# Weight-stationary jobs of a two-layer hybrid decoder: three products of 256 columns per k tile in one PSUM bank, in place of 512 and 256 columns in two

## The chip, the cores and the metric

The kernel runs on one core of a Trainium2 chip, in one launch. The metric is the device time of one execution in microseconds (us). The kernel before takes 1260.89 us (median of 3 runs, 1260.34 to 1261.17). Matrix products run on TensorE (PE in the profile; its weight loads are PEld), elementwise work on VectorE (DVE), ScalarE (ACT) and GpSimd (POOL). SyncE (SP) issues most loads. PSUM is the memory that TensorE writes to, in banks of 128 x 512 float32.

## The reference

Two layers over 256 tokens of width 1024. Each layer has a mixer and a SwiGLU network, both on RMS-normed input, both added to the running h:

```
def hybrid_mixer(h, w_in, ...):
    u = h @ w_in
    q, k, v, g_ret, z, xbc, dt, gate_ret, gate_ssd = split(u)
    qf, kf = rotary(q), rotary(k) * DK ** -0.5
    yr = silu(g_ret) * norm(retention(qf, kf, v))
    o_ret = yr @ ret_out
    xbc = silu(causal_dwconv(xbc, conv_w, conv_b))
    xs, bm, cm = split(xbc)
    ys = ssd_scan(xs * dtp, dtp * a, bm, cm) + d_skip * xs
    o_ssd = (groupnorm(ys * silu(z)) * ssd_norm_w) @ ssd_out
    return (sigmoid(gate_ret) * o_ret + sigmoid(gate_ssd) * o_ssd) @ w_o

def swiglu(h, w_gate_up, w_down):
    gate, up = split(h @ w_gate_up)
    return (silu(gate) * up) @ w_down
```

A last RMSNorm follows. All is float32. There are 4 retention heads (256 wide q and k, 512 wide v), 32 SSD heads in 4 groups, and the SwiGLU width is 2816.

## The kernel before

**Products in three parts.** A float32 operand is split into a high part, rounded to float32r, and the low rest, and a product is the sum of three: high by high, high by low, low by high (`mm3`, L538). Activations are split once. Weights are split after they land, 128 x 1024 elements at a time, in `split_piece` (L490): ScalarE rounds `wh` (L502), VectorE takes `wl = raw - wh` (L523). A pair wh, wl occupies one of `HB` = 6 split slots (semaphore `hlS`, L258) from the rounding until its last product. Raw tiles (`RB` = 4) are loaded by SP in a fixed order (`feeder`, L474). In some jobs a sum of two weight tiles is made by a GpSimd DMA that adds in place (L412).

**Two kinds of job on TensorE.** In a tm job (`tm_jobs`, L801) tokens are stationary: the 128 x 128 weights of the array come from the transposed activations, and 512 columns of wh or wl stream past, with the lines L539, L540, L541 of `mm3`. The jobs `seven` (L840) do the same with seven products for eight (Strassen's scheme). In an fm job (`fm_job`, L944) the weight tile is stationary and the 256 tokens stream, so that the output stands channel by row: q and k (for the rotary turn), the convolution's channels (xs and bc), and three blocks of the SwiGLU. There are 30 fm jobs in a layer, 60 in all. Each makes 256 channels as two blocks (b) of 128, and each block runs over 8 k tiles. The activation tile holds high and low part side by side, `x = [xh | xl]`, so that one matmul of 512 columns does wh by both:

```
if k < 7:
    nc.tensor.matmul(a, lhsT=wh[..], rhs=x[..], ...)           # L962, 512 columns
nc.tensor.matmul(a[:, :SEQ], lhsT=wl[..], rhs=xh[..], ...)     # L963, 256 columns
if k == 7:
    nc.tensor.matmul(a, lhsT=wh[..], rhs=x[..], ...)           # L965, 512 columns
```

A block thus fills a whole bank: the left half has wh xh + wl xh, the right half wh xl. `gathered` (L980) adds the halves: ScalarE copies the right one out, VectorE adds the left one, and the bank is released. This is done for block 0 while block 1 runs. Then come the steps of the job's kind: `rotary` (L1357, VectorE), `conv` (L1456: one ScalarE step and three VectorE steps per block, then one Silu), or `gate` and `up` of `fm_pair` (L1830). A variant `fm_direct` (L920) with three products of 256 columns is in the code and is used by no job (`DIRECT = ()`, L1120).

**What sets the order.** All engines' queues are written out by a planner that runs when the kernel is built (`Flow`, L72). Every step is a stream that yields operations with an engine, a cost in ns and a priority (the smaller goes first); the planner simulates the engines with these costs and emits each operation when its engine would take it. So a cost or a delay in the planner changes only the order in which instructions stand in the queues. On the chip each engine takes its queue strictly in that order and waits where an operand isn't there. There are 6 banks for products (`accS`, L255), 2 for transposes (`trS`, L256) and 2 large scratch tiles (`ccS`, L259).

**Around the merge.** At the end of `ssd_out`, `ssd_post` (L1743) gates each 128 x 512 block of the sum on VectorE (`D<-acc,D`), adds the retention branch (`D<-D`), and `transposed` (L627) lets TensorE transpose it (L636) for the product with `w_o`, whose first products follow. `transposed` has an argument `slack`: a delay in the planner, after the transpose bank is taken, before TensorE is asked; some callers give `SLOW` = 1500 ns. In `z_job` (L1712) the sums for the seven products of `ssd_out` have the priority of the job plus `ZS_PR` = 1.0.

Of the kernel before, what the change touches and what calls it, by code (L numbers as in the profile page):

```python
# [11 lines left out]
AF = mybir.ActivationFunctionType  # L12
ALU = mybir.AluOpType
# [179 lines left out]
def trunk_kernel(  # L193
# [3 lines left out]
    ssd_out, w_o, norm_ffn_w, w_gate_up, w_gf, w_sw, w_dw, w_down, final_norm_w, consts, out,  # L197
):
    nc = tc.nc
    HB, RB, TAIL, WARM = 6, 4, 5, 2  # L200
    APART, LATE = (), 2500.0
    SLOW = 1500.0
    ZS_PR = 1.0
    PR0, SLACK = 1.6, 2500.0
    BESIDE = (8, 10, 12, 14, 11, 11, 9, 24, 44)
    APARTS, SUMS_PR = {}, 3.5
# [21 lines left out]
    def tt(n, pr, out, in0, in1, op):  # L228
        return dve(n, pr, lambda: nc.vector.tensor_tensor(out=out, in0=in0, in1=in1, op=op))  # L229
# [14 lines left out]
    def pe(cost, pr, fn):  # L244
        return Op("pe", cost, fn, pr)

    def mm_cost(n, fp32=False):
        return n * 4 / 2.4 + 4 if fp32 else max(n / 2.4 + 13.4, 110)
# [668 lines left out]
        for q in jobs[j]:  # L917
            yield from product(q)

    def fm_direct(xT, post):  # L920

        j, pe_pr = take()
        evs = jobs[j]
        box = []
        yield accS
        for b in range(2):
            fsl, to = slice(b * P, (b + 1) * P), slice(b * SEQ, (b + 1) * SEQ)
            for k in range(8):
                for t in range(NT):
                    yield xT.ready[k // 4][t]  # L930
                wh, wl = yield evs[k // 4]

                def emit():
                    if not box:
                        box.append(new_acc())
                    xh, xl = xT.at(k // 4)[:2]
                    mm3(box[0][:, to], wh[:, k % 4, fsl], wl[:, k % 4, fsl], xh[:, k % 4, :], xl[:, k % 4, :], k == 0, k == 7)

                yield pe(3 * mm_cost(256), pe_pr + 0.5, emit)
                if b == 1 and k % 4 == 3:  # L940
                    fl.release(hlS)
        fl.spawn(post(box[0], None, j))

    def fm_job(xT, post):  # L944

        j, pe_pr = take()
        evs = jobs[j]
        second = Event()
        for b in range(2):
            fsl = slice(b * P, (b + 1) * P)  # L950
            yield accS
            ps = None
            for k in range(8):
                for t in range(NT):
                    yield xT.ready[k // 4][t]
                wh, wl = yield evs[k // 4]

                def emit():
                    a = new_acc() if ps is None else ps
                    xh, _, x = xT.at(k // 4)  # L960
                    if k < 7:
                        nc.tensor.matmul(a, lhsT=wh[:, k % 4, fsl], rhs=x[:, k % 4, :, :], start=k == 0, stop=False)  # L962
                    nc.tensor.matmul(a[:, :SEQ], lhsT=wl[:, k % 4, fsl], rhs=xh[:, k % 4, :], start=False, stop=False)  # L963
                    if k == 7:
                        nc.tensor.matmul(a, lhsT=wh[:, k % 4, fsl], rhs=x[:, k % 4, :, :], start=False, stop=True)  # L965
                    return a

                ps = yield pe(mm_cost(512) + mm_cost(256) + 5, pe_pr + 0.5, emit)
                if b == 1 and k % 4 == 3:
                    fl.release(hlS)  # L970
            if b == 0:
                fl.spawn(post(ps, second, j))
            else:
                fl.set(second, ps)

    def halves(a):
        a = a.rearrange("p (i b t) -> p i b t", i=2, b=2)
        return a[:, 0, :, :], a[:, 1, :, :]

    def gathered(ps, u, pr):  # L980

        yield act(SEQ, pr, u, ps[:, SEQ:], AF.Copy, psum=True)
        yield tt(SEQ, pr, u, ps[:, :SEQ], u, ALU.add)
        fl.release(accS)

    def out_job(op, nk, post, head=0):

# [43 lines left out]
    def out_wino(op, nk, at, tag, order, post, add, ops):  # L1031
# [72 lines left out]
        for t in range(NT):  # L1104
# [12 lines left out]
           [("fm", 3)],  # L1117
           [("seven", (4,), ("t3", "t4"))],
           [("fm", NPAIR)]]
    DIRECT = ()  # L1120
    DOWN_APART = ()


# [75 lines left out]
    def layer(l, mix, nxt, opening=None):  # L1199
# [155 lines left out]
        ret_ev = [Event() for _ in range(RH)]  # L1355

        def rotary(dst, done):  # L1357
            def post(ps, second, j):
                d = yield dst
                yield ccS  # L1360
                tcx, tsx = halves(new_cc())
                yield from gathered(ps, tcx[:, 0, :], j)
                ps = yield second
                yield from gathered(ps, tcx[:, 1, :], j)
                yield tt(512, j, tsx, tcx, sin.unsqueeze(1).broadcast_to([P, 2, SEQ]), ALU.mult)
                yield tt(512, j, tcx, tcx, cos.unsqueeze(1).broadcast_to([P, 2, SEQ]), ALU.mult)
# [86 lines left out]
        run["q"], run["k"] = q_job, k_job  # L1453


        def conv(ps, second, blk, dst, pr):  # L1456
            cv, _ = yield par
            yield ccS
            u, cvt = halves(new_cc())

            def col(i, b):
                return cv[:, i, blk + b : blk + b + 1]

            for b in range(2):
                if b:
                    ps = yield second
                yield from gathered(ps, u[:, b, :], pr)
                yield act(SEQ, pr, cvt[:, b, :], u[:, b, :], AF.Identity, scale=col(3, b), bias=col(4, b))
                for i in range(1, 4):
                    yield stt(SEQ - i, pr, cvt[:, b, i:], u[:, b, : SEQ - i], col(3 - i, b), cvt[:, b, i:], ALU.mult, ALU.add)  # L1470
            yield act(512, pr, dst, cvt, AF.Silu)
            fl.release(ccS)

# [1 line left out]
        bc_ev = [[Event(), Event()] for _ in range(2)]  # L1475

        def bc_post(w, jj):
            def post(ps, second, j):
# [4 lines left out]
                yield from conv(ps, second, 16 + 4 * w + 2 * jj, d[:, 2 * jj : 2 * jj + 2, :], j)  # L1483
                fl.set(bc_ev[w][jj])
            return post

# [11 lines left out]
        cb_left = [SG]  # L1498

        def xs_post(g, jj):  # L1500
            def post(ps, second, j):
# [6 lines left out]
                yield from conv(ps, second, 4 * g + 2 * jj, sT, j)  # L1508
                yield trS
                yield SLOW  # L1510

# [231 lines left out]
        def ssd_post(t, n, ps, j):  # L1743
            nsl = slice(n * 512, (n + 1) * 512)
            yield sgs_ev[t][n]
            yield tt(512, j - 1, sgs[t][:, nsl], ps, sgs[t][:, nsl], ALU.mult)
            fl.release(accS)
            yield mr_ev[t][n]
            yield tt(512, j - 1, sgr[t][:, nsl], sgr[t][:, nsl], sgs[t][:, nsl], ALU.add)
            yield from transposed(sgr[t][:, nsl], 4, mT, n, t, j - 1)  # L1750
            if n == 1:
                fl.release(bigS["D"])
                fl.release(bigS["D"])
# [76 lines left out]
        def fm_pair(c):  # L1830
# [3 lines left out]
            for half in range(left[0]):  # L1834
                gated = Event()

                def summed(ps, second, u, j):
                    for b in range(2):
                        if b:
                            ps = yield second  # L1840
                        yield from gathered(ps, u[:, b * SEQ : (b + 1) * SEQ], j)

                def gate(ps, second, j, gated=gated):
                    yield silS
                    s = new_sil()
                    if second is None:
                        yield act(512, j, s, ps, AF.Silu, psum=True)
                        fl.release(accS)
                    else:
                        yield from summed(ps, second, s, j)  # L1850
                        yield act(512, j, s, s, AF.Silu)
                    fl.set(gated, s)

                def up(ps, second, j, gated=gated, half=half):
                    if second is None:
                        s = yield gated
                        yield tt(512, j, s, ps, s, ALU.mult)
                        fl.release(accS)
                    else:
                        yield sxS  # L1860
                        u = new_sx()
                        yield from summed(ps, second, u, j)
                        s = yield gated
                        yield tt(512, j, s, u, s, ALU.mult)
                        fl.release(sxS)
                    yield from gu.take(c)
                    dh, dl = (a[:, 2 * half : 2 * half + 2, :] for a in gu.at(c)[:2])
                    v = s.rearrange("p (b t) -> p b t", b=2)
# [5 lines left out]
                        for t in range(NT):  # L1874
                            fl.set(gu.ready[c][t])

                job = fm_direct if c in DIRECT else fm_job
                makers += [((lambda p=p, job=job: job(ffn.xT, p)), 1) for p in (gate, up)]
            return makers

        def pair(c):
# [211 lines left out]
```

## Time and profile before

| | before |
|---|---|
| median of 3 runs | 1260.89 us |
| profiled execution, its own time | 1260.23 us |
| its span, first to last instruction | 1258.2 us |
| VectorE busy | 1062.3 us, 84% |
| ScalarE busy | 851.0 us, 68% |
| granted TensorE clock, mean | 0.999 |

A matmul's record lasts longer than the array is taken by it, since matmuls overlap in the pipeline: records of 512 columns last 400 ns and start every 227 ns or so. How long TensorE is taken by a matmul is therefore read from the distance between starts (the pitch), and idle time of TensorE below some 0.17 us does not show in the busy sums. In the rows of the timeline the first two numbers are start and length in us; neighbours of the same kind are merged into one row with their count.

### The profile page before, as it was taken

Reading aid. Unit: us, or ns where it says so; the run is one execution under the profiler, and the core shown is the slowest. Engines: PE = TensorE matmul, PEld = TensorE weight load, DVE = VectorE, ACT = ScalarE, POOL = GpSimd, SP = SyncE. Lnnn points to the kernel's source line nnn. Section 1 sums busy time; section 2 is a strip of 40 time slices with the busy share of each in tenths; the row PEclk is TensorE's granted clock in tenths of the full one; section 3 lists DMA queues with packets and bytes.
Section 4 is the critical chain, followed back from the end, with each engine's and each line's share of the span. In section 5 each row is a group of like instructions: output and inputs, shape, how many; then the busy total and the mean of one; then the engine's idle time right before and its main releaser. Section 6 shows DMA issues by size and latency. Waiting matters only on the chain.

```text
span 1258.2 us, 17517 instructions
## 1 busy us (share of the span) xinstructions
PE 1247.1 (99%) x6306; PEld 1055.3 (84%) x6306; DVE 1062.3 (84%) x1452; ACT 851.0 (68%) x1271; POOL 64.4 (5%) x84
## 2 busy tenths in 40 slices
PE   9999999999999999999999999999999999999997
PEld 7889888888888788888888898888888887888886
DVE  6998978878589978999788888878875998888996
ACT  6876786987376566776586676967954664766754
POOL 0000000000012001011000000000000110010010
PEclk9999999999999999999999999999999999999999
DMA  8668555555475757886766485555555765678873
GB/s 292 222 176 292 178 175 160 175 189 196 154 281 148 230 177 225 296 225 207 229 210 226 123 266 166 172 192 167 187 199 170 242 189 201 206 226 254 271 202 113
DMA packets 73606, 258.13 MB, mean 205 GB/s; under 512 B 8464, under 2 KB 8720, under 8 KB 73520
## 3 DMA queue, kind: packets, MB, share of 16 engines
q1 hardware_dynamic: 66832, 233.32, 54.6%
q0 software_dynamic: 6400, 23.18, 9.8%
q8 instruction: 49, 0.80, 0.2%
q10 hardware_dynamic: 288, 0.52, 0.1%
q14 instruction: 37, 0.30, 0.1%
HBM read 255.88 MB, written 1.11 MB: 204 GB/s over the span
## 4 chain that ended last, share of the span: by engine, by line
PE 86%; DVE 8%; DMA 3%; issue 2%; ACT 1%; SPq 0%; POOL 0%; POOLq 0%; ACTq 0%; DVEq 0%
PE acc L540 17%; PE acc L539 17%; PE acc L541 17%; PE acc L962 16%; PE acc L963 9%; DVE wl L523 4%; PE tr L636 2%; PE acc L965 2%; PE yps L1623 2%; DVE raws L229 1%; DMA raws<-in_w_sw_dram 1%; DMA raw<-in_w_dw_dram 1%; DMA raw<-in_ssd_out_dram 1%; DVE D L229 1%; DVE plain L229 1%
## 5 line engine op out<-in xcount | busy, mean ns | idle before, releaser
L523 DVE TENSOR_TENSOR wl<-raw,wh 128x1024 fp32r<-128x1024 f32 (+2 forms) x392 | 464.5, 1194 | 76.1 <-ACT wh L502 73.7
L502 ACT ACTIVATE wh<-raw 128x1024 fp32r<-128x1024 f32 (+2 forms) x392 | 400.9, 1036 | 186.2 <-PE acc L541 87.3
L962 PE MATMUL acc<-xT,wh 128*128 128x512 f32 x840 | 304.1, 400 | 0.0
L963 PE MATMUL acc<-xT,wl 128*128 128x256 f32 x960 | 252.2, 281 | 0.0
L539 PE MATMUL acc<-wh,xT 128*128 128x512 f32 (+1 forms) x568 | 219.5, 386 | 0.0
L541 PE MATMUL acc<-wh,xT 128*128 128x512 f32 (+1 forms) x568 | 216.0, 380 | 0.0
L540 PE MATMUL acc<-wl,xT 128*128 128x512 f32 (+1 forms) x568 | 216.0, 380 | 0.0
L963 PEld LDWEIGHTS acc<-xT,wl 128*128 128x128 f32 x960 | 181.2, 189 | 10.1
L962 PEld LDWEIGHTS acc<-xT,wh 128*128 128x128 f32 x840 | 158.0, 188 | 32.3
L540 PEld LDWEIGHTS acc<-wl,xT 128*128 128x128 f32 x568 | 106.7, 188 | 20.1 <-issue 1.0
L539 PEld LDWEIGHTS acc<-wh,xT 128*128 128x128 f32 x568 | 106.7, 188 | 19.5 <-issue 1.2
L541 PEld LDWEIGHTS acc<-wh,xT 128*128 128x128 f32 x568 | 106.7, 188 | 19.5
L502 ACT ACTIVATE wh<-raws 128x1024 fp32r<-128x1024 f32 x80 | 84.1, 1057 | 45.1 <-DVE raws L229 23.6
L523 DVE TENSOR_TENSOR wl<-raws,wh 128x1024 fp32r<-128x1024 f32 x80 | 96.3, 1218 | 9.2 <-ACT wh L502 9.1
L539 PE MATMUL acc<-wh,A 128*128 128x512 f32 x224 | 89.0, 397 | 0.0
L541 PE MATMUL acc<-wh,A 128*128 128x512 f32 x224 | 87.3, 390 | 0.0
L540 PE MATMUL acc<-wl,A 128*128 128x512 f32 x224 | 87.2, 389 | 0.0
L232 DVE SCALAR_TENSOR_TENSOR cc<-cc,cv 128x255 f32<-128x255 f32 (+1 forms) x144 | 68.3, 477 | 11.5 <-ACT cc L222 10.4
L539 PE MATMUL acc<-wh,C 128*128 128x512 f32 (+1 forms) x184 | 72.2, 392 | 0.0
L540 PE MATMUL acc<-wl,C 128*128 128x512 f32 (+1 forms) x184 | 71.2, 387 | 0.5 <-DVE wl L523 0.3
L541 PE MATMUL acc<-wh,C 128*128 128x512 f32 (+1 forms) x184 | 70.7, 384 | 0.0
L541 PEld LDWEIGHTS acc<-wh,A 128*128 128x128 f32 x224 | 42.1, 188 | 9.0
(183 smaller groups left out, 1889.0 us busy)
## 6 DMA issues: line engine op xcount, KB each, us to landing
raw<-in_w_tm_dram SPq DMA_DIRECT2D x104, 512.0 KB, 4.2
raw<-in_w_fm_dram SPq DMA_DIRECT2D x80, 512.0 KB, 4.0
raw<-in_w_gf_dram SPq DMA_DIRECT2D x40, 512.0 KB, 4.7
raw<-in_ret_out_dram SPq DMA_DIRECT2D x32, 512.0 KB, 3.8
raw<-in_w_gate_up_dram SPq DMA_DIRECT2D x32, 512.0 KB, 6.0
raw<-in_w_down_dram SPq DMA_DIRECT2D x28, 512.0 KB, 4.4
raw<-in_w_gr_dram SPq DMA_DIRECT2D x24, 352.0 KB, 3.8
seg<-acs SPq DMA_DIRECT2D x16, 512.0 KB, 5.1
```

What stands on the lines that cost most here:

```text
L229: return dve(n, pr, lambda: nc.vector.tensor_tensor(out=out, in0=in0, in1=in1, op=op))
L232: return Op("dve", 1.04 * n + 130, lambda: nc.vector.scalar_tensor_tensor(out=out, in0=in0, scalar=scalar, in1=in1, op0=op0, op1=op1), pr)
L502: nc.scalar.activation(out=wh[:, :m], in_=raw[:, :m], func=AF.Copy)
L523: nc.vector.tensor_tensor(out=wl[:, :m], in0=raw[:, :m], in1=wh[:, :m].bitcast(F32), op=ALU.subtract)
L539: nc.tensor.matmul(ps, lhsT=lh, rhs=rh, start=first, stop=False, **kw)
L540: nc.tensor.matmul(ps, lhsT=lh, rhs=rl, start=False, stop=False, **kw)
L541: nc.tensor.matmul(ps, lhsT=ll, rhs=rh, start=False, stop=last, **kw)
L636: nc.tensor.transpose(out=ps[:, j * P : (j + 1) * P], in_=src[:, j * P : (j + 1) * P], identity=ident)
L962: nc.tensor.matmul(a, lhsT=wh[:, k % 4, fsl], rhs=x[:, k % 4, :, :], start=k == 0, stop=False)
L963: nc.tensor.matmul(a[:, :SEQ], lhsT=wl[:, k % 4, fsl], rhs=xh[:, k % 4, :], start=False, stop=False)
L965: nc.tensor.matmul(a, lhsT=wh[:, k % 4, fsl], rhs=x[:, k % 4, :, :], start=False, stop=True)
L1623: nc.tensor.matmul(ps[:, i * HD : (i + 1) * HD], lhsT=sg[:, i, :], rhs=xdt[:, i * HD : (i + 1) * HD], start=True, stop=True)
```

## The change

- `fm_job` and `gathered` go; `fm_direct` takes the name `fm_job` and does all 60 jobs. Each k tile is wh xh, wh xl, wl xh of 256 columns each, all into one half of one bank; block 1 uses the other half. The step that reads the result is spawned once, after both blocks. The planner's cost of a k tile is 3 * 117 = 351 ns (for the pair before: 352).
- The steps read the bank itself: `rotary` multiplies by sin and cos from PSUM, `conv` reads PSUM in its ScalarE step and its three VectorE steps per block, `gate` and `up` read PSUM. The bank is released after the last of these reads.
- `HB` goes from 6 to 7 split slots (8 KB more in each partition), and the scratch memory for the descriptors of GpSimd's DMAs is set to 8192 bytes (`dynamic_dma_scratch_size`).
- The transposes of the merged sum get `slack = MT_SLACK` = 800 ns.
- `ZS_PR` goes from 1.0 to 0.5.

```
-    HB, RB, TAIL, WARM = 6, 4, 5, 2
+    HB, RB, TAIL, WARM = 7, 4, 5, 2
-    SLOW = 1500.0
-    ZS_PR = 1.0
+    SLOW, MT_SLACK = 1500.0, 800.0
+    ZS_PR = 0.5
...
-    def fm_direct(xT, post):
+    def fm_job(xT, post):
         j, pe_pr = take()
         evs = jobs[j]
         box = []
         yield accS
         for b in range(2):
             fsl, to = slice(b * P, (b + 1) * P), slice(b * SEQ, (b + 1) * SEQ)
             for k in range(8):
...
                     xh, xl = xT.at(k // 4)[:2]
                     mm3(box[0][:, to], wh[:, k % 4, fsl], wl[:, k % 4, fsl], xh[:, k % 4, :], xl[:, k % 4, :], k == 0, k == 7)
-                yield pe(3 * mm_cost(256), pe_pr + 0.5, emit)
+                yield pe(3 * 117, pe_pr + 0.5, emit)
                 if b == 1 and k % 4 == 3:
                     fl.release(hlS)
-        fl.spawn(post(box[0], None, j))
+        fl.spawn(post(box[0], j))
...
-    def gathered(ps, u, pr):
-        yield act(SEQ, pr, u, ps[:, SEQ:], AF.Copy, psum=True)
-        yield tt(SEQ, pr, u, ps[:, :SEQ], u, ALU.add)
-        fl.release(accS)
...
         def rotary(dst, done):
-            def post(ps, second, j):
+            def post(ps, j):
                 d = yield dst
                 yield ccS
                 tcx, tsx = halves(new_cc())
-                yield from gathered(ps, tcx[:, 0, :], j)
-                ps = yield second
-                yield from gathered(ps, tcx[:, 1, :], j)
-                yield tt(512, j, tsx, tcx, sin.unsqueeze(1).broadcast_to([P, 2, SEQ]), ALU.mult)
-                yield tt(512, j, tcx, tcx, cos.unsqueeze(1).broadcast_to([P, 2, SEQ]), ALU.mult)
+                x = ps.rearrange("p (b t) -> p b t", b=2)
+                yield tt(512, j, tsx, x, sin.unsqueeze(1).broadcast_to([P, 2, SEQ]), ALU.mult)
+                yield tt(512, j, tcx, x, cos.unsqueeze(1).broadcast_to([P, 2, SEQ]), ALU.mult)
+                fl.release(accS)
...
-        def conv(ps, second, blk, dst, pr):
+        def conv(ps, blk, dst, pr):
             cv, _ = yield par
             yield ccS
-            u, cvt = halves(new_cc())
+            _, cvt = halves(new_cc())
+            u = ps.rearrange("p (b t) -> p b t", b=2)
...
             for b in range(2):
-                if b:
-                    ps = yield second
-                yield from gathered(ps, u[:, b, :], pr)
-                yield act(SEQ, pr, cvt[:, b, :], u[:, b, :], AF.Identity, scale=col(3, b), bias=col(4, b))
+                yield act(SEQ, pr, cvt[:, b, :], u[:, b, :], AF.Identity, psum=True, scale=col(3, b), bias=col(4, b))
                 for i in range(1, 4):
                     yield stt(SEQ - i, pr, cvt[:, b, i:], u[:, b, : SEQ - i], col(3 - i, b), cvt[:, b, i:], ALU.mult, ALU.add)
+            fl.release(accS)
             yield act(512, pr, dst, cvt, AF.Silu)
...
-            yield from transposed(sgr[t][:, nsl], 4, mT, n, t, j - 1)
+            yield from transposed(sgr[t][:, nsl], 4, mT, n, t, j - 1, slack=MT_SLACK)
...
-                def up(ps, second, j, gated=gated, half=half):
-                    if second is None:
-                        s = yield gated
-                        yield tt(512, j, s, ps, s, ALU.mult)
-                        fl.release(accS)
-                    else:
-                        yield sxS
-                        u = new_sx()
-                        yield from summed(ps, second, u, j)
-                        s = yield gated
-                        yield tt(512, j, s, u, s, ALU.mult)
-                        fl.release(sxS)
+                def up(ps, j, gated=gated, half=half):
+                    s = yield gated
+                    yield tt(512, j, s, ps, s, ALU.mult)
+                    fl.release(accS)
...
-    nc = _bacc.Bacc("TRN2", target_bir_lowering=False, num_devices=1)
+    nc = _bacc.Bacc("TRN2", target_bir_lowering=False, num_devices=1, dynamic_dma_scratch_size=8192)
```

More of the change, by code (lines that the diff above doesn't have):

```diff
@@ L937, in emit @@
                     mm3(box[0][:, to], wh[:, k % 4, fsl], wl[:, k % 4, fsl], xh[:, k % 4, :], xl[:, k % 4, :], k == 0, k == 7)
-                yield pe(3 * mm_cost(256), pe_pr + 0.5, emit)
+                yield pe(3 * 117, pe_pr + 0.5, emit)
                 if b == 1 and k % 4 == 3:
                     fl.release(hlS)
-        fl.spawn(post(box[0], None, j))
[L944 to L972, printed above, removed]
-            else:
-                fl.set(second, ps)
+        fl.spawn(post(box[0], j))
     def halves(a):
@@ L1119, in trunk_kernel @@
            [("fm", NPAIR)]]
-    DIRECT = ()
     DOWN_APART = ()
@@ L1477, in bc_post, with post @@
         def bc_post(w, jj):
-            def post(ps, second, j):
+            def post(ps, j):
                 if jj == 0:
@@ L1482, in post @@
                 d = yield bc[w]
-                yield from conv(ps, second, 16 + 4 * w + 2 * jj, d[:, 2 * jj : 2 * jj + 2, :], j)
+                yield from conv(ps, 16 + 4 * w + 2 * jj, d[:, 2 * jj : 2 * jj + 2, :], j)
                 fl.set(bc_ev[w][jj])
@@ L1500, in xs_post, with post @@
         def xs_post(g, jj):
-            def post(ps, second, j):
+            def post(ps, j):
                 if jj == 0:
@@ L1507, in post @@
                 sT = new_sx("sT").rearrange("p (b t) -> p b t", b=2)
-                yield from conv(ps, second, 4 * g + 2 * jj, sT, j)
+                yield from conv(ps, 4 * g + 2 * jj, sT, j)
                 yield trS
@@ L1835, in fm_pair, with gate @@
                 gated = Event()
[L1837 to L1843, printed above, removed]
+                def gate(ps, j, gated=gated):
                     yield silS
                     s = new_sil()
-                    if second is None:
-                        yield act(512, j, s, ps, AF.Silu, psum=True)
-                        fl.release(accS)
-                    else:
-                        yield from summed(ps, second, s, j)
-                        yield act(512, j, s, s, AF.Silu)
-                    fl.set(gated, s)
-                def up(ps, second, j, gated=gated, half=half):
-                    if second is None:
-                        s = yield gated
-                        yield tt(512, j, s, ps, s, ALU.mult)
-                        fl.release(accS)
-                    else:
-                        yield sxS
-                        u = new_sx()
-                        yield from summed(ps, second, u, j)
-                        s = yield gated
-                        yield tt(512, j, s, u, s, ALU.mult)
-                        fl.release(sxS)
+                    yield act(512, j, s, ps, AF.Silu, psum=True)
+                    fl.release(accS)
+                    fl.set(gated, s)
+                def up(ps, j, gated=gated, half=half):
+                    s = yield gated
+                    yield tt(512, j, s, ps, s, ALU.mult)
+                    fl.release(accS)
                     yield from gu.take(c)
@@ L1875, in up @@
                             fl.set(gu.ready[c][t])
-                job = fm_direct if c in DIRECT else fm_job
-                makers += [((lambda p=p, job=job: job(ffn.xT, p)), 1) for p in (gate, up)]
+                makers += [((lambda p=p: fm_job(ffn.xT, p)), 1) for p in (gate, up)]
             return makers
```

## The prediction

> **What bounds the kernel now.** First the busy sums and the same sums by stretch: is one engine full, and where is it not?
>
> ```profile
> span 1258.2 us, 17517 instructions
> PE 1247.1 (99%) x6306; PEld 1055.3 (84%) x6306; DVE 1062.3 (84%) x1452; ACT 851.0 (68%) x1271; POOL 64.4 (5%) x84
> 0.00:25.00 25.00, 23.44 (x109) 19.10 (x110) 14.32 (x27) 14.82 (x28) 0.76 (x5) 1.00 0.85 287
> ...
> 400.00:425.00 25.00, 23.94 (x109) 19.61 (x108) 24.00 (x28) 15.61 (x17) 1.72 (x2) 1.00 0.73 214
> ...
> 1025.00:1050.00 25.00, 24.07 (x110) 19.40 (x109) 23.84 (x29) 14.31 (x17) 0.21 (x1) 1.00 0.77 244
> ...
> 1250.00:1275.00 25.00, 1.19 (x6) 0.65 (x4) 2.23 (x5) 1.66 (x5) 0.55 (x1) 0.88 0.06 21
> ```
>
> After each stretch stand its length and the busy time of PE, PEld, DVE, ACT and POOL. TensorE is idle for 1258.2 - 1247.1 = 11.1 us. Of these 7.0 (8.2 - 1.19) are the last norm, which the change does not touch, 1.6 the start, 1.1 and 0.9 the two merges with w_o. The rest of the span is TensorE's own work, so a microsecond on VectorE or ScalarE is worth nothing by itself, and the pitch of the matmuls is worth everything. The fm jobs' share is large:
>
> ```profile
> L962 PE MATMUL acc<-xT,wh 128*128 128x512 f32 x840 | 304.1, 400 | 0.0
> L963 PE MATMUL acc<-xT,wl 128*128 128x256 f32 x960 | 252.2, 281 | 0.0
> L965 PE MATMUL acc<-xT,wh 128*128 128x512 f32 x120 | 47.6, 397 | 0.0
> ```
>
> That is 960 k tiles, each with one matmul of 512 and one of 256 columns. Their pitch is in the timeline of steady stretches: a tm job with 512 columns, one with 352, and an fm job.
>
> ```profile
> 417.80 0.39 PE L539 MATMUL acc<-wh,C 128*128 128x512 f32 x1
> ...
> 422.56 0.39 PE L539 MATMUL acc<-wh,C 128*128 128x512 f32 x1
> ```
> ```profile
> 109.75 0.32 PE L539 MATMUL acc<-wh,xT 128*128 128x352 f32 x1
> ...
> 113.90 0.32 PE L541 MATMUL acc<-wh,xT 128*128 128x352 f32 x1
> ```
> ```profile
> 1104.91 0.40 PE L963 MATMUL acc<-xT,wl 128*128 128x256 f32 x2
> 1105.14 0.40 PE L965 MATMUL acc<-xT,wh 128*128 128x512 f32 x1
> 1105.38 0.40 PE L962 MATMUL acc<-xT,wh 128*128 128x512 f32 x1
> ...
> 1108.20 0.40 PE L962 MATMUL acc<-xT,wh 128*128 128x512 f32 x1
> ...
> 1110.55 0.40 PE L963 MATMUL acc<-xT,wl 128*128 128x256 f32 x2
> 1110.78 0.40 PE L965 MATMUL acc<-xT,wh 128*128 128x512 f32 x1
> 1111.02 0.40 PE L962 MATMUL acc<-xT,wh 128*128 128x512 f32 x1
> ```
>
> Twenty-one starts lie between the two 512 rows: 4.76 / 21 = 0.2267 us. Twenty-six lie between the 352 rows: 4.15 / 26 = 0.1596 us. The rows at 1105.38, 1108.20 and 1111.02 are three starts of a block of 8 k tiles: 5.64 / 16 = 0.3525 us for a k tile of 512 and 256 columns.
>
> **The change part by part.**
>
> *The k tile on TensorE.* 768 columns stream before and after. What changes is their division, two matmuls into three, and the number of weight loads, two into three (wh is loaded twice in a row). The trace has one place where two matmuls of 256 columns stand one behind the other, each with its own weight load: L963 of k = 6 and of k = 7, the rows with x2. To the start of L965 behind them there are 0.23 us (1104.91 to 1105.14, and 1110.55 to 1110.78), with rows rounded to 0.01, so 115 to 117.5 ns for each. I take 117 ns, the upper end, since a long run has no 512-column matmul to catch up in: 3 x 117 = 351 ns against 352.5, that is -1.5 ns x 960 = **-1.4 us**. From below, 115 ns gives 345 and -7.2 us. From above there are two readings, which are the rivals below: 119.3 ns (+5.3 us) and 126 ns (+24 us). I choose the middle because it is the only row of the very form that the new job has.
>
> The Trainium skill ("TensorE: Matmul & The Clock Gate", Back-to-back issue gap) speaks against the division: it has a fixed cost of about 2.5 ns for each warm matmul above its columns, so one more matmul in each of 960 k tiles would be an estimated +2.4 us. The trace's 0.2267 us for 512 columns is some 13 ns above 512 / 2.4, so what is added here is larger than the page's, and the rows above decide.
>
> *What leaves VectorE and ScalarE.* `gathered` ran 120 times on each:
>
> ```profile
> L229 DVE TENSOR_TENSOR cc<-acc,cc 128x256 f32<-128x256 f32 x80 | 33.2, 417 | 10.2 <-ACT cc L222 10.1
> L229 DVE TENSOR_TENSOR sx<-acc,sx 128x256 f32<-128x256 f32 x20 | 8.4, 418 | 4.5 <-ACT sx L222 4.5
> L229 DVE TENSOR_TENSOR sil<-acc,sil 128x256 f32<-128x256 f32 x20 | 8.3, 417 | 0.0
> L229 DVE TENSOR_TENSOR C<-cc 128x256 f32<-128x256 f32 x32 | 12.6, 416 | 0.1
> L232 DVE SCALAR_TENSOR_TENSOR cc<-cc,cv 128x255 f32<-128x255 f32 x48 | 23.0, 479 | 10.6 <-ACT cc L222 10.4
> L222 ACT ACTIVATE cc<-acc 128x256 f32<-128x256 f32 x80 | 29.9, 375 | 13.4 <-PE acc L965 13.2 <-PE y L541 0.2
> L222 ACT ACTIVATE cc<-cc,cv 128x256 f32<-128x256 f32 x48 | 28.5, 596 | 26.9 <-DVE cc L229 26.9
> ```
>
> VectorE loses 33.2 + 8.4 + 8.3 = 49.9 us of records. The steps that stay now read PSUM, which the 256-column rows price the same as SBUF (417 ns from acc, 416 ns from cc), so nothing comes back. ScalarE loses 29.9 and, by the same 0.375 us, 40 more, 45 us in all. None of this is on TensorE's path, so it counts only through waits for `wl` and for a free bank. Outside the start, the merges and the end the stretches show about half a microsecond of idle TensorE, and records of 0.39 us at a pitch of 0.227 hide waits below some 0.16 us each. A seventh split slot and 50 us less on VectorE can remove part of that: I take **-0.8 us**, between 0 and -3.
>
> *The seventh slot* lets the splits run one tile further ahead:
>
> ```profile
> ACT wh L502 <- PE acc L541: 92.9, 62, 9.8
> q0 software_dynamic: 6400, 23.18, 9.8%
> ```
>
> ScalarE waits 92.9 us for TensorE to give a slot back: the splits are ahead of TensorE most of the time already, so a slot more buys little. Raw tiles come free sooner and SP's loads start sooner; their number and order in SP's queue stay. The smaller descriptor memory concerns the 6400 packets of GpSimd's queue. What a smaller ring costs is in no row; nothing to lose if its adds are issued in time, and if the second of two adds had to wait for the landing of the first, its weights would come some 5 to 8 us later. I take nothing, because that queue fills 9.8%.
>
> *The later start of the steps.* Block 0 was gathered while block 1 ran; now all begins after both, 8 x 0.351 = 2.8 us later for the first half, and saves two gathers. Behind a step wait the rotated q and k (scores), the convolved channels (transposes, SSD) and the gated halves. The planner knows this and puts other jobs' products ahead, as it does now, so I cost it at nothing. One bank is held for 16 x 0.351 = 5.6 us and some 5 us of steps, at one job in 5.6 us: two banks of six. If a wide job beside it lacked a bank, TensorE would wait for the rest of a convolution, 1 to 3 us, at a few places.
>
> *The merge.* At each merge one transpose stands in TensorE's queue before its operand is there:
>
> ```profile
> 423.01 0.39 PE L541 MATMUL acc<-wh,C 128*128 128x512 f32 x1
> 423.63 0.68 DVE L229 TENSOR_TENSOR D<-D 128x512 f32<-128x512 f32 x1
> 424.46 0.63 PE L636 MATMUL tr<-cst,D 128*128 128x128 f32 x4 [1.06 <-DVE D L229]
> ...
> 1044.65 0.39 PE L541 MATMUL acc<-wh,C 128*128 128x512 f32 x1
> 1045.13 0.68 DVE L229 TENSOR_TENSOR D<-D 128x512 f32<-128x512 f32 x1
> 1045.96 0.63 PE L636 MATMUL tr<-cst,D 128*128 128x128 f32 x4 [0.92 <-DVE D L229]
> ```
>
> From the last matmul to the transpose are 1.45 and 1.31 us, less a pitch of 0.227: 1.22 and 1.08 us lost. A delay of 0.8 us in the planner lets one more part of three matmuls (0.68 us) go first, so each wait shrinks by about 0.8: **-1.6 us** for both, between 0 (the order falls as badly again) and -2.3 (all). What waits for the transposes, the first products of w_o, has 12 parts of 0.68 us, or 8 us, ahead of the one that needs the last block, so a delay of 0.8 is covered; uncovered, it would cost 0.8 at each. `ZS_PR` moves VectorE's sums for ssd_out ahead of other steps of the same time; no TensorE wait at that place is seen, so nothing.
>
> *The sum.* -1.4 - 0.8 - 1.6 = -3.8 us against the profiled execution's 1260.23 us, which is 0.7 below the median 1260.89. Taken off the median: **1257.1 us**, -0.30%. A measurement of this kernel tells a difference from about 0.2%, or 2.5 us.
>
> **The rivals.**
>
> *A fixed cost for each matmul (slower).* The two tm pitches give a slope of (226.7 - 159.6) / 160 = 0.419 ns for a column, and for 256 columns 159.6 - 96 x 0.419 = 119.3 ns. Then a k tile takes 358 ns, +5.5 x 960 = +5.3 us, and with the -2.4 of the other parts the time is 1263.8 us, +0.23%. For it: two clean rows. Against it: the rows of the form itself (115 to 117.5). It decides from (352.5 + 5.1) / 3 = 119.2 ns on, where the loss of 4.9 us outweighs the other parts by 2.5. The skill's fixed cost, named above, is of this kind, only smaller.
>
> *Weight loads that don't fit (much slower).* If a 512-column matmul takes 226.7 ns in an fm job too, the pair's 352.5 leaves 126 ns for 256 columns with the load of the next weights under it. Three of those are 378 ns, +24 us: 1283 us. The rows of small matmuls give the pitch of loads alone:
>
> ```profile
> 194.90 1.90 PE L1623 MATMUL yps<-xdt,seg 128*128 128x64 f32 x16
> 196.63 0.61 PE L1516 MATMUL tr<-cst,sT 128*128 128x128 f32 x4
> ```
>
> 1.73 / 16 = 0.108 us each, though only 64 columns stream: a load takes about that, just below 117. So it fits, barely, and I give this little.
>
> *The 256-column form is faster than I read.* 115 ns on average: -7.2 - 2.4 = -9.6, 1251.3 us. The same rows allow it.
>
> *The side parts don't do what they say.* Other job lengths reorder all queues; the merge's wait may come back elsewhere, or a wait for a bank take its place. Then the -2.4 is lost and up to 3 us added: 1259.5 to 1262.5 us.
>
> **How the numbers follow.** Forecast (116 to 118 ns, side parts mostly as summed): 0.45, nearly all of it faster. Faster form: 0.13, faster. Fixed cost: 0.22, about half within 0.2%. Side parts fail: 0.14, two thirds within. Loads: 0.06, slower. Faster by over 0.2%: 0.40 + 0.13 + 0.02 = 0.55. Within: 0.05 + 0.11 + 0.10 = 0.26. Slower: 0.11 + 0.02 + 0.06 = 0.19. The range goes from 1248 (a part more than the faster form) to 1265 (the fixed cost and a small new wait) and leaves out the loads and the tails of the others. The forecast's own range is 1255 to 1259.
>
> **What would show it.** In the profile after: starts of a block of 8 k tiles 2.81 us apart (351 ns a k tile) say the first step is right, 2.86 the fixed cost, 3.0 the loads. The gather rows on both engines are gone and the records of the convolution stay near 479 and 596 ns. TensorE's idle before the merge's transposes falls from 1.06 + 0.92 us to below 1 in all. If idle time stands before the L540 kind of line with a releaser on VectorE, or before a job's first matmul with the release of a bank, the steps' later start was not covered. A pitch above 119.2 ns, or GpSimd's adds landing late, would make the prediction wrong.

## The result, and the profile after

The changed kernel is slower: 1271.45 us (median of 5 runs, 1270.28 to 1274.51) against 1260.89 us, a ratio of 1.0090 with a 95% interval of 1.0080 to 1.0101. That is +10.6 us, where -3.8 us was forecast, and outside the range of 1248 to 1265 us. The profiled execution is the longest of the five, 1274.51 us.

The page of the changed kernel, its span and busy sums:

```profile
span 1272.7 us, 19141 instructions
PE 1257.3 (99%) x7266; PEld 1108.1 (87%) x7266; DVE 1024.3 (80%) x1332; ACT 816.0 (64%) x1149; POOL 66.4 (5%) x84
```

VectorE and ScalarE do lose work (1062.3 to 1024.3 us, 851.0 to 816.0 us of busy time), and the span grows by 14.5 us. TensorE's busy sum grows by 10.2 us, its idle time by 4.3 us (1272.7 - 1257.3 = 15.4, against 11.1). Most of both has a place.

The first is the pitch. The groups of TensorE by form show the new job, and the timeline (start, length) a steady piece of it:

```profile
L539 PE MATMUL acc<-xT,wh 128*128 128x256 f32 x960 | 275.4, 287 | 0.0
L541 PE MATMUL acc<-xT,wl 128*128 128x256 f32 x960 | 271.5, 283 | 0.0
L540 PE MATMUL acc<-xT,wh 128*128 128x256 f32 x960 | 271.5, 283 | 0.0
```
```profile
1119.81 0.28 PE L540 MATMUL acc<-xT,wh 128*128 128x256 f32 x1
...
1121.01 0.28 PE L541 MATMUL acc<-xT,wl 128*128 128x256 f32 x1
```

Between the last two rows lie ten starts: 1.20 / 10 = 120 ns. A k tile of three takes 360 ns, where the old pair took 352.5 and the forecast had 351. For 960 k tiles that is +7.2 us.

The second is one place in the first layer. The 25 us stretches there, first of the kernel before, then of the changed one, columns as before (length, PE, PEld, DVE, ACT, POOL busy, granted clock):

```profile
75.00:100.00 25.00, 24.75 (x126) 20.87 (x125) 23.86 (x31) 17.94 (x25) 0.88 (x1) 1.00 0.65 168
100.00:125.00 25.00, 25.00 (x144) 22.83 (x143) 20.55 (x24) 17.08 (x23) 0.00 (x0) 1.00 0.83 290
```

```profile
75.00:100.00 25.00, 23.84 (x130) 20.14 (x129) 21.13 (x29) 15.66 (x21) 0.88 (x1) 1.00 0.62 152
100.00:125.00 25.00, 21.42 (x113) 19.23 (x112) 18.03 (x19) 16.07 (x21) 0.00 (x0) 0.93 0.77 260
```

4.7 us of idle TensorE stand in these 50 us, where the kernel before has 0.25. In the same stretch the granted clock falls to 0.93, the only such drop between the start and the end; by an estimate from that figure it costs 0.07 x 25, some 1.7 us, and these stand in the busy sum. The timeline of TensorE and of ScalarE there, with the idle time before a row and what ended it in brackets:

```profile
104.82 0.32 PE L541 MATMUL acc<-wh,xT 128*128 128x352 f32 x1
108.22 0.52 PE L539 MATMUL acc<-wh,xT 128*128 128x512 f32 x1 [3.08 <-ACT D L222]
108.56 0.61 PE L540 MATMUL acc<-wl,xT 128*128 128x512 f32 x1
108.96 0.63 PE L541 MATMUL acc<-wh,xT 128*128 128x512 f32 x1
109.39 0.49 PE L539 MATMUL acc<-wh,xT 128*128 128x352 f32 x1
```
```profile
105.60 0.79 ACT L502 ACTIVATE wh<-raw 128x704 fp32r<-128x704 f32 x1 [0.42 <-DMA raw<-in_w_gr_dram]
106.41 1.28 ACT L222 ACT_TABLE_LOAD   x1
107.70 0.82 ACT L222 ACTIVATE D<-acc 128x352 f32<-128x352 f32 x2
```

A matmul of 512 columns waits 3.08 us for `D<-acc`, the Sigmoid step of a merge gate's job. What such a step gives to TensorE is the PSUM bank that it has read. The step stands in ScalarE's queue behind a weight split that waits for its load, and behind a table load. After the wait 512 columns take 0.40 to 0.43 us (108.56 to 108.96, to 109.39) instead of 0.227.

The merge with w_o is as it was, 1.0 us of wait (0.88 shows as idle) in spite of the delay:

```profile
433.69 0.39 PE L541 MATMUL acc<-wh,C 128*128 128x512 f32 x1
434.96 0.63 PE L636 MATMUL tr<-cst,D 128*128 128x128 f32 x4 [0.88 <-DVE D L229]
```

### The profile page after: what moved, and what is told of

It reads as the page before. It is cut to its first block, busy times and chain, and to the rows that moved or that the text cites. A ratio compares the mean times of both kernels' runs of the same rounds, so it can differ in the third digit from the quotient of the medians.

```text
span 1272.7 us, 19141 instructions
## 1 busy us (share of the span) xinstructions
PE 1257.3 (99%) x7266; PEld 1108.1 (87%) x7266; DVE 1024.3 (80%) x1332; ACT 816.0 (64%) x1149; POOL 66.4 (5%) x84
## 4 chain that ended last, share of the span: by engine, by line
PE 86%; DVE 5%; DMA 5%; issue 2%; ACT 1%; SPq 0%; POOL 0%; POOLq 0%; ACTq 0%; DVEq 0%
PE acc L539 26%; PE acc L541 26%; PE acc L540 26%; DVE wl L523 3%; PE tr L636 2%; PE yps L1582 2%; DMA raw<-in_w_tm_dram 2%; DMA raws<-in_w_sw_dram 1%; ACT wh L502 1%; PE tr L1475 1%; PE acc L1343 1%; PE ips L1569 1%; DMA raw<-in_w_gr_dram 0%; DVE sx L229 0%; PE y L539 0%
## 5 line engine op out<-in xcount | busy, mean ns | idle before, releaser
L539 PE MATMUL acc<-xT,wh 128*128 128x256 f32 x960 | 275.4, 287 | 0.0
L541 PE MATMUL acc<-xT,wl 128*128 128x256 f32 x960 | 271.5, 283 | 0.0
L540 PE MATMUL acc<-xT,wh 128*128 128x256 f32 x960 | 271.5, 283 | 0.0
L540 PEld LDWEIGHTS acc<-xT,wh 128*128 128x128 f32 x960 | 183.9, 192 | 1.4 <-issue 0.5
L539 PEld LDWEIGHTS acc<-xT,wh 128*128 128x128 f32 x960 | 183.9, 192 | 1.4 <-issue 0.5
L541 PEld LDWEIGHTS acc<-xT,wl 128*128 128x128 f32 x960 | 183.8, 192 | 0.0
L232 DVE SCALAR_TENSOR_TENSOR cc<-acc,cv,cc 128x255 f32<-128x255 f32 (+1 forms) x144 | 68.0, 477 | 10.3 <-ACT cc L222 9.5
L539 PE MATMUL acc<-wh,C 128*128 128x512 f32 (+1 forms) x184 | 71.9, 391 | 0.0
```

What stands on the lines that cost most here:

```text
L232: return Op("dve", 1.04 * n + 130, lambda: nc.vector.scalar_tensor_tensor(out=out, in0=in0, scalar=scalar, in1=in1, op0=op0, op1=op1), pr)
L539: nc.tensor.matmul(ps, lhsT=lh, rhs=rh, start=first, stop=False, **kw)
L540: nc.tensor.matmul(ps, lhsT=lh, rhs=rl, start=False, stop=False, **kw)
L541: nc.tensor.matmul(ps, lhsT=ll, rhs=rh, start=False, stop=last, **kw)
```

## The experiments

Theory 1 is that a matmul has a fixed cost of some 13 ns on top of its columns, so that three of 256 cost more than 512 and 256. Against it stand theory 2, that the side parts (seventh slot, descriptor memory, delay, priority) made the loss, and theory 3, that the steps' later start did. Each time is the median, with the ratio to runs of the kernel before on the same chip.

**The three products alone.**

```
-    HB, RB, TAIL, WARM = 7, 4, 5, 2
+    HB, RB, TAIL, WARM = 6, 4, 5, 2
-    SLOW, MT_SLACK = 1500.0, 800.0
-    ZS_PR = 0.5
+    SLOW, MT_SLACK = 1500.0, 0.0
+    ZS_PR = 1.0
-    nc = _bacc.Bacc("TRN2", ..., dynamic_dma_scratch_size=8192)
+    nc = _bacc.Bacc("TRN2", ...)
```

> The three products and the reading from the bank alone: 6 split slots, no delay at the merge, ZS_PR 1.0 and the descriptor memory of before. Theory 1 (pitch): nearly all of the +10.6 us is the pitch of 120 ns for 256 columns, so this kernel has +8 to +9 us (1269 to 1270 us) and 960 k tiles at 360 ns. Theory 2 (side parts): the seventh slot, the small descriptor memory or the delay brought the wait at 91 to 112 us of the span; then it is gone here, and the time is 1269 at most. Theory 3 (later steps): that wait comes from the steps that begin after both blocks; then it is here too, and the time is 1270 to 1273 us.

1266.81 us against 1260.26, ratio 1.0054 (1.0037 to 1.0071): +6.6 us. Theory 3 falls: there is no wait near 105 us. The time is 2 to 3 us less than theory 1 expected and 4 to 5 us below the full change, and it lies where theory 2 put it. So the pitch explains this kernel, but not nearly all of the +10.6 us. The stretches of this kernel:

```profile
75.00:100.00 25.00, 24.94 (x137) 21.54 (x137) 23.17 (x31) 17.21 (x22) 0.87 (x1) 1.00 0.62 162
100.00:125.00 25.00, 25.00 (x167) 24.03 (x166) 20.54 (x23) 17.11 (x22) 0.00 (x0) 1.00 0.85 291
```

**The side parts alone**, on the kernel before.

```
-    HB, RB, TAIL, WARM = 6, 4, 5, 2
+    HB, RB, TAIL, WARM = 7, 4, 5, 2
-    ZS_PR = 1.0
+    ZS_PR = 0.5
-    yield from transposed(sgr[t][:, nsl], 4, mT, n, t, j - 1)
+    yield from transposed(sgr[t][:, nsl], 4, mT, n, t, j - 1, slack=800.0)
+    ... dynamic_dma_scratch_size=8192
```

> The kernel before with 7 split slots, 8192 bytes of descriptor memory, the delay of 800 ns at the merge and ZS_PR 0.5; the old k tiles. Theory 1: within 1.5 us of before (1259.5 to 1262.5 us), the merge's waits of 1.2 and 1.1 us as before or smaller. Theory 2: slower by 2 us or more (1263 us and up), with a wait of TensorE near 90 to 110 us. The prediction's sum for these parts was -2.4 us (1258.5 us).

1260.35 us against 1260.26, ratio 1.0003 (0.9994 to 1.0013). The side parts alone cost nothing and bring nothing. So the change is not the sum of its two halves: +6.6 and +0.1 against +10.6.

**Which side part it is.** Two kernels take single parts out of the full change: one has 6 slots, the other no delay and the old priority.

```
-    HB, RB, TAIL, WARM = 7, 4, 5, 2        # after_hb6
+    HB, RB, TAIL, WARM = 6, 4, 5, 2
```
```
-    SLOW, MT_SLACK = 1500.0, 800.0         # after_hb7
-    ZS_PR = 0.5
+    SLOW, MT_SLACK = 1500.0, 0.0
+    ZS_PR = 1.0
```

> The changed kernel with 6 split slots instead of 7, all else as changed (8192 bytes of descriptor memory, delay of 800 ns, ZS_PR 0.5). The changed kernel was 4 to 5 us above the three products alone (1271.4 and 1266.8 us). If the seventh slot, with the queue order that it makes, is what adds them, this is 1266 to 1268 us and TensorE's wait of 3 us near 105 us is gone; if the descriptor memory, the delay or the priority does, it stays at 1270 to 1272 us.

> The changed kernel without the delay at the merge and with ZS_PR 1.0 as before, but with 7 slots and the small descriptor memory. If the seventh slot (or the descriptor memory) adds the 4 to 5 us, 1270 to 1272 us with the wait near 105 us; if the delay and the priority do, 1266 to 1268 us.

With 6 slots: 1267.06 against 1259.66, ratio 1.0059 (1.0044 to 1.0074), the time of the products alone. With 7 slots and neither delay nor priority: 1272.25, ratio 1.0100 (1.0085 to 1.0115), the time of the full change. The loss of 4 to 5 us belongs to the seventh slot together with the new jobs; the small descriptor memory is in both and costs nothing that shows. The same stretch with 6 slots, and the wait with 7:

```profile
100.00:125.00 25.00, 25.00 (x169) 24.11 (x168) 19.58 (x23) 17.24 (x22) 0.00 (x0) 1.00 0.84 292
```
```profile
106.54 0.79 PE L539 MATMUL acc<-wh,xT 128*128 128x512 f32 x1 [2.57 <-ACT D L222]
107.13 0.63 PE L540 MATMUL acc<-wl,xT 128*128 128x512 f32 x1
107.56 0.63 PE L541 MATMUL acc<-wh,xT 128*128 128x512 f32 x1
```

**The wait for the bank.** If the Sigmoid step is late because it stands behind a split, an earlier place helps.

```
-                yield act(352 - lo, j, sgr[t][:, o : o + 352 - lo], ps[:, lo:352], AF.Sigmoid, ...)
+                yield act(352 - lo, j - 1.5, sgr[t][:, o : o + 352 - lo], ps[:, lo:352], AF.Sigmoid, ...)
```

> The changed kernel, all parts, with one priority altered: the Sigmoid step of the merge gates' jobs (ScalarE, D<-acc) is put 1.5 ahead in the planner, so that it stands in ScalarE's queue before the weight splits of the next such job. If TensorE's wait of 3.1 us near 105 us is for the bank that this step frees, and the step is late because it stands behind a split that waits for its weights' landing, the wait goes and the time falls to that of 6 slots: 1266 to 1268 us. If the wait is for weights or for the raw tiles, it stays: 1270 to 1272 us.

1272.18 us against 1259.94, ratio 1.0097 (1.0080 to 1.0114): no gain. The profiled execution took 1269.85 us, the other three 1271.96 to 1273.13, and these have no trace. In it the step stands ahead of one split that it stood behind, and the wait is there still, 2.03 us long. That this is shorter than the 3.08 us of the changed kernel is no clear gain: that trace is of an execution of 1274.51 us, 3 us above its kernel's median. The rows of TensorE, then of ScalarE:

```profile
105.20 0.50 PE L539 MATMUL acc<-wh,xT 128*128 128x512 f32 x1 [2.03 <-ACT D L222]
105.54 0.39 PE L540 MATMUL acc<-wl,xT 128*128 128x512 f32 x1
105.77 0.40 PE L541 MATMUL acc<-wh,xT 128*128 128x512 f32 x1
```
```profile
103.39 1.28 ACT L222 ACT_TABLE_LOAD   x1
104.68 0.82 ACT L222 ACTIVATE D<-acc 128x352 f32<-128x352 f32 x2
```

So the split in front is not the whole of it: the table load (1.28 us) and the step itself still lie between the gate's last product and the bank. In all three kernels with the wait TensorE's queue has seven k tiles of 352 columns of the gate's job in a row ahead of the place; with 6 slots these alternate with the 512-column products of the other job. There the Sigmoid step too stands behind a split and a table load (at 105.23 us), and TensorE has other products meanwhile. A row of such tiles does not make the wait by itself: with 6 slots sixteen stand in a row from 107.55 us on, and TensorE does not wait. That the order with seven slots uses up the banks is argued from the queues and not shown by a run.

**The pitch by itself.** Behind the last fm job of the changed kernel stand nine runs of 24 matmuls into a spare bank, each with its own weight load. They are additional work and change no output. The pitches are from one execution.

```
+        for i in range(24):
+            nc.tensor.matmul(a[:, :256], **mm(i, 256))
+        for i in range(24):
+            nc.tensor.matmul(a[:, :512], **mm(i, 512))
+        for i in range(24):
+            nc.tensor.matmul(a[:, : 256 if i % 2 else 512], **mm(i, 256 if i % 2 else 512))
+        for i in range(24):
+            nc.tensor.matmul(a[:, : 256 if i % 4 in (1, 2) else 512], ...)
...
```

> The changed kernel with nine runs of 24 matmuls into a spare bank behind its last weight-stationary job, each with its own weight load; only their pitch matters. A fixed cost of 13.3 ns on top of N / 2.4: 66.7 or the load's 109 for 128, 109 for 192 (bound by the load), 120 for 256, 146.7 for 320, 173.3 for 384, 226.7 for 512. A cost in proportion to the columns (17/16): 113 for 256, 142 for 320, 170 for 384, 227 for 512. A load that does not fit under 256 columns: 120 for 256 but no rise from 192 to 256. Alternating 512 and 256: 346.7 a pair if the parts add, 352 to 353 if the mixture itself costs; 512, 256, 256, 512 then shows whether the order does.

The timeline, one row for a run; the rows are in the order 256, 512, 512 and 256 in turn, 512-256-256-512, 384, 320, 192, 128, and 256 with the same weights each time:

```profile
1205.15 3.04 PE L932 MATMUL bench<-xT,wh 128*128 128x256 f32 x24
1208.03 5.63 PE L934 MATMUL bench<-xT,wh 128*128 128x512 f32 x24
1213.50 4.39 PE L936 MATMUL bench<-xT,wh 128*128 128x512 f32 x24
1217.73 4.35 PE L938 MATMUL bench<-xT,wh 128*128 128x512 f32 x24
1221.92 4.35 PE L940 MATMUL bench<-xT,wh 128*128 128x384 f32 x24
1226.11 3.67 PE L942 MATMUL bench<-xT,wh 128*128 128x320 f32 x24
1229.62 2.82 PE L944 MATMUL bench<-xT,wh 128*128 128x192 f32 x24
1232.28 2.81 PE L946 MATMUL bench<-xT,wh 128*128 128x128 f32 x24
1234.92 3.08 PE L948 MATMUL bench<-xT,wh 128*128 128x256 f32 x24
```

The distance of two rows by 24 is the pitch: 120.0 ns for 256 columns, 228 for 512, 175 for 384, 146 for 320, and 111 and 110 for 192 and 128. From 256 up this is N / 2.4 + 13.3 ns (120.0, 146.7, 173.3, 226.7) within 1.4 ns. It is a fixed cost, not one in proportion (113 for 256 columns). 192 and 128 columns take the same, so there is a floor of some 110 ns; where it takes over lies between 192 and 256 columns, by the line at some 232 (an estimate, no width between was run). Each matmul here has a weight load of its own, so whether the 13 ns belong to the matmul or to the load is not separated. 512 and 256 in turn take 4.23 / 12 = 352.5 ns a pair, the old pair's time, although the parts add up to 346.7: the mixture has a cost of its own, 6 ns. So the new k tile pays 13.3 ns for one more matmul and is rid of these 6, which leaves the 7.5 ns between 352.5 and 360. And 512-256-256-512 takes 4.19 / 12 = 349 ns a pair, the order of the next kernel.

**The old pair in turned order.** The kernel before, with 512 and 256 columns exchanged in every odd k tile:

```
-                    if k < 7:
+                    if k % 2 == 0:
                         nc.tensor.matmul(a, lhsT=wh[..], rhs=x[..], start=k == 0, stop=False)
                     nc.tensor.matmul(a[:, :SEQ], lhsT=wl[..], rhs=xh[..], start=False, stop=False)
-                    if k == 7:
-                        nc.tensor.matmul(a, lhsT=wh[..], rhs=x[..], start=False, stop=True)
+                    if k % 2:
+                        nc.tensor.matmul(a, lhsT=wh[..], rhs=x[..], start=False, stop=k == 7)
```

> The kernel before with the order of the two matmuls turned round in every odd k tile (512, 256, 256, 512, ...). If the 6 ns by which the old pair (352.5) is above 226.7 + 120 come with each step from 256 to 512 columns, half of those steps are gone: about -3 ns for 960 k tiles, -3 us (1258 us). If they belong to the 512-column matmul of this form itself, nothing changes (within 1 us of before).

1257.00 us against 1260.26, ratio 0.9979 (0.9969 to 0.9988): -3.3 us, as expected from a cost of each step between widths; the run after this one shows that the reason is another. It is faster than both kernels. The timeline, first and last start of 16 k tiles:

```profile
1103.19 0.40 PE L965 MATMUL acc<-xT,wh 128*128 128x512 f32 x1
...
1108.76 0.40 PE L965 MATMUL acc<-xT,wh 128*128 128x512 f32 x1
```

5.57 / 16 = 348 ns a k tile, 4.4 below the old pair, or -4.2 us for 960 of them.

**Fewer changes still:** the matmuls of a block in the order 4 of 512, 8 of 256, 4 of 512.

```
-            for k in range(8):
+            for wide, k in [(w, k) for w, ks in ((1, range(4)), (0, range(4)), (0, range(4, 8)), (1, range(4, 8))) for k in ks]:
...
+                    if wide:
+                        nc.tensor.matmul(a, lhsT=wh[..], rhs=x[..], start=k == 0, stop=k == 7)
+                    else:
+                        nc.tensor.matmul(a[:, :SEQ], lhsT=wl[..], rhs=xh[..], start=False, stop=False)
```

> The kernel before with the old matmuls of a block in the order 4 of 512, 8 of 256, 4 of 512 columns. Same matmuls, fewer changes of width (alternate has one for each matmul pair, before two). If each change of width costs some 3 ns, a k tile comes near 226.7 + 120 = 346.7 ns, that is 5 to 7 ns below before and 2 to 4 below alternate: 1254 to 1256 us. If the gain of alternate was something else (the two neighbours of 256 columns themselves), the time is at 1257 us or above.

1256.60 us against 1259.66, ratio 0.9975 (0.9966 to 0.9985): as fast as the turned order, not faster, and between the two cases expected. The idea of a cost for each change of width falls, since this kernel has a quarter of the turned order's changes. Its timeline:

```profile
1102.90 1.12 PE L964 MATMUL acc<-xT,wl 128*128 128x256 f32 x8
1103.86 2.00 PE L962 MATMUL acc<-xT,wh 128*128 128x512 f32 x8
1105.70 1.11 PE L964 MATMUL acc<-xT,wl 128*128 128x256 f32 x8
```

Eight of 256 take 0.96 us, eight of 512 1.84 us: 2.80 / 8 = 350 ns a k tile, where a cost of 3 ns for each change would have made 347 to 348. The distances of the starts, in ns from the trace, tell why single distances mislead:

```
256 columns: 113 119 120 120 120 120 120 120
512 columns: 233 236 228 233 231 226 227 227
```

The first two of a run of 256 follow early, and the first five of 512 behind them pay back more than that. Only the sum over a whole period is a price.

**A longer delay at the merge**, on the turned order:

```
-    SLOW = 1500.0
+    SLOW, MT_SLACK = 1500.0, 2500.0
```

> The alternating order of the old pair (1257.0 us) with a delay of 2500 ns at the merge. If the merge's two waits of about 1 us come from the planner asking for the transposes too early, a delay three times that of the change takes most of both away: 1255 to 1256 us. If VectorE's queue is what is late there (a weight split between the two steps of the merge), the transposes only move and the waits stay near 1 us: 1257 us.

1261.26 us against 1259.66, ratio 1.0015 (1.0006 to 1.0025): some 4 us slower than without the delay, and outside both cases expected. The transposes no longer wait; the first products of w_o do, which need them, 4.1 us in both layers:

```profile
424.68 1.19 PE L636 MATMUL tr<-cst,D 128*128 128x128 f32 x8
427.12 0.50 PE L539 MATMUL acc<-wh,A 128*128 128x512 f32 x1 [1.24 <-ACT A L222]
428.69 0.50 PE L541 MATMUL acc<-wh,A 128*128 128x512 f32 x1 [0.84 <-DVE A L229]
```

With 800 ns the result depends on the rest of the queue: in the full change the transposes wait 1.8 us in all, with 6 slots 0.2 us, without the delay 1.6 us (the three products alone), and no time shows the difference. The lines of the full change and of 6 slots:

```profile
L636 PE MATMUL tr<-cst,D 128*128 128x128 f32 x32 | 4.8, 274 | 1.8 <-DVE D L229 1.8
```
```profile
L636 PE MATMUL tr<-cst,D 128*128 128x128 f32 x32 | 4.8, 274 | 0.2 <-DVE D L229 0.2
```

## Why the prediction was wrong

**What bounds the kernel** was read rightly: 38 and 35 us less on VectorE and ScalarE brought nothing that a run shows, and the pitch decided. (The prediction's 49.9 and 45 us are sums of records, and the gathers' rows are gone; the busy time falls by less because it counts overlapping records once.)

**The k tile on TensorE is the step that failed.** The prediction took 117 ns, because two neighbours of 256 columns in the old job were "the only row of the very form". They are not: they are the first two of a run, behind a 512-column matmul, and a long run settles at 120. Such a pair lies 113 and 119 ns apart in the list above, and the 512-column matmuls behind it are stretched. The step should have priced a period, or trusted the line through the two steady jobs, which gave 119.3. The term was -1.4 us; with 120 ns it is +7.2, and the three products alone measured +6.6. The rival "a fixed cost for each matmul" had the mechanism, and its 119.3 ns were 0.7 too low, but it got a chance of only 0.22. Its 1263.8 us counts the -2.4 of the other parts; without them it is 1266.2, close to the 1266.8 of the three products alone.

The kernel before held the right price, which the prediction passed over. Its planner costs a matmul by `max(n / 2.4 + 13.4, 110)` (`mm_cost`, L247): 120.1 ns for 256 columns, 360 for three. Its old pair has 5 ns on top of the two parts, 352. The change put 3 * 117 in place of 3 * `mm_cost(256)`, and the same 117 went into the forecast. All kernels with the new job plan with it; whether the order with seven slots is better when planned with 360, no run tests.

The rival of the weight loads took the pair's whole surplus (126 ns) for the price of 256 columns. The bench refutes it: 120 ns, and the surplus of 6 ns belongs to the mixture.

**The seventh slot** was costed at next to nothing. Alone that is right (1.0003). With the new jobs it makes an order in which TensorE waits up to 3 us in the first layer, by the queues for a bank, and runs slowly for a while behind the wait; 4 to 5 us are lost. This is the rival "the side parts don't do what they say", with a wait for a bank in place of the one removed, at a place that the prediction did not name, and together with the fixed cost instead of alone. The range's upper end, 1265 us, did put a wait on top of the fixed cost, but a small one of about 1 us, with the -2.4 us of gains kept; the gains did not come and the wait cost 4 to 5 us.

**The merge** (-1.6 us) and **the waits for wl** (-0.8 us) brought nothing measurable. The prediction said that 8 us of products cover a delay of 0.8 us. With 6 slots this held: the transposes' wait falls to 0.2 us and no wait of w_o's products comes in its place, yet the time does not fall by an amount that a run shows. A delay of 2500 ns is not covered: w_o's first products waited 1.24 and 0.84 us in the first layer. **The reads from PSUM** were priced rightly: the convolution's steps stay at 479 ns, and ScalarE's reads got shorter, 559 ns for 596.

```profile
L232 DVE SCALAR_TENSOR_TENSOR cc<-acc,cv,cc 128x255 f32<-128x255 f32 x48 | 23.0, 479 | 9.6 <-ACT cc L222 9.5
L222 ACT ACTIVATE cc<-acc,cv 128x256 f32<-128x256 f32 x48 | 26.8, 559 | 19.8 <-DVE cc L232 9.8 <-PE acc L541 9.8
```

**The later start of the steps** cost nothing that shows, as said: with 6 slots TensorE has no idle time in the stretch from 100 to 125 us.

## What to carry to other kernels

Where TensorE is full, count its matmuls as well as its columns: dividing the same columns into more matmuls cost 13 ns for each one more here, and the relief of other engines did not pay for it. When a change overwrites a cost that the code already holds, ask why the two differ. Price a matmul by whole periods of a steady run, never by the distance of two starts next to a matmul of another width. A part that is free alone is not free beside another: an order written by a planner changes as a whole, so test the parts singly and together.

## What the runs showed of the hardware

Mixing widths costs: 512 and 256 columns in turn take 352.5 ns where the separate runs add up to 346.7, and a mere exchange of every second pair takes 4.4 ns off a k tile and 3.3 us off the kernel. What in TensorE makes it, no run shows.

After a wait of 3.08 us TensorE ran at about half its speed for a while (0.40 to 0.43 us for 512 columns, clock 0.93 in that stretch), and so it did with seven slots and no delay after a wait of 2.57 us (0.43 us from 107.13 to 107.56, clock 0.93 from 100 to 125 us); after one of 2.03 us it did not (0.23 us). The Trainium skill ("TensorE: Matmul & The Clock Gate", Why this matters for your kernels) warns of idle gaps over about 3 us, behind which the clock is halved. The waits of 3.08 and 2.03 us agree with it, but the one of 2.57 us is shorter than that figure and had the clock halved as well. The measurement decides: here a wait below 3 us was enough, and three waits do not give the limit.
